# Soft-routed experts on one core: the first 512 rows of x by SP in float32, cast by ScalarE and VectorE

## The chip, the cores and the metric

The kernel runs on one core of a Trainium2 chip. Its engines are TensorE (PE: matmuls; PEld are its weight loads), VectorE (DVE), ScalarE (ACT), GpSimd (POOL) and SyncE (SP, which only issues DMAs). PE reads its operands from the on-chip memory SBUF and writes to PSUM, which has eight banks of 128 x 512 float32; DVE and ACT carry results from there. DMAs that SP issues go through the hardware queue q1, those that POOL issues through the software queue q0, for which POOL itself prepares the descriptors; only POOL's DMAs change the data type on the way. The metric is the device time in microseconds (us) of one execution.

## The reference, cut to what matters

```python
probs = softmax(router_logits)            # 16 x 512 tokens, 8 experts
output = zeros((16, 512, 2048))           # float32
for e in range(8):
    output += probs[:, :, e:e+1] * (x @ expert_weights[e])   # x: 512 columns, weights 512 x 2048
```

So every token's row of x is scaled by a probability and multiplied with each expert's weights; the eight products are summed.

## The kernel before

Tokens are taken flat, 8192 of them. The scaled rows z = p * x in float16, side by side for all experts, make one large matrix product, which the kernel computes with seven products in place of eight at two levels (Strassen's scheme in Winograd's form). A stage of it is `sub_product` (L370): for 256 rows at a time it multiplies sums of z blocks with sums of weight blocks and keeps the results in HBM; the last stage (from L607) puts the output together.

The change lies in the opening, before the first `sub_product`. There the kernel computes the first 512 rows' product with one quarter of the weights (`b11`, experts 0 to 3 and columns 0 to 1023) plainly:

- L94 to L104: DVE clears a tile, and PE runs 13 warm-up matmuls on zeros (`every`).
- L214 to L232: `xs0` is a float16 tile for 1024 rows of x, eight blocks of 128 x 512. `load_lg0(0)` brings the first logits by SP. `cast_x(0)` and `cast_x(2)` bring rows 0 to 255 and 512 to 767 by POOL, each one DMA from float32 in HBM to float16 in SBUF.
- L234 to L236: the identity matrix; POOL cuts it out of ones with `affine_select`.
- L237 to L245: POOL's queue then brings the weights `b11`: block (0,0) of expert 0 in two halves, the rest of the first three blocks in five DMAs of 512 KB (counted in float16), then `cast_x(4)`, `cast_x(6)`, then the fourth block. `behind()` keeps them after what was issued before on each engine's own queue.
- L247 to L274: `early_p` is the softmax of the first logits. `diag_e(e)` makes four diagonal matrices of expert e's probabilities, on DVE. `early_z0(e, d)` multiplies each 128-row block of xs0 with such a diagonal on PE, which transposes and scales it in one step: 4 blocks j of 4 matmuls, each block to one bank. `evacuate` casts the bank to the z tile `z0[j]`: DVE takes j = 0 and 2, ACT j = 1 and 3.
- L437 to L466: the order of the opening, which is kept as written for DVE and ACT (`keep_in_program_order` in the helper at L114):

```python
    ds_ = [diag_e(0), diag_e(1)]
    early_z0(0, ds_[0])
    ds_.append(diag_e(2))
    load_logits()
    early_z0(1, ds_[1])
```

After these lines come the two column halves n: for n = 0 the remaining `early_z0(2)` and `early_z0(3)` stand before the main matmuls of experts 0 and 1, and the main matmuls of expert e multiply z0[j][e] with the block `b11[e // 2, n]`. `load_logits` (L301) clears an element of each of two tiles on DVE, on which SP's loads of the other logits wait. SP carries one queue of its own; POOL issues its DMAs in the order of the text, and each waits until the DMA eight places ahead of it in POOL's queue has landed.

Of the kernel before, what the change touches and what calls it, by code (L numbers as in the profile page):

```python
# [32 lines left out]
def kernel(  # L33
# [7 lines left out]
    nc = tc.nc  # L41
    P = 128
    f16 = mybir.dt.float16
    f32 = mybir.dt.float32
# [3 lines left out]
    B, S, H = x.shape  # L48
# [7 lines left out]
    HQ = 256  # L56
# [4 lines left out]
    x_f = x.flatten_outer_dims()  # L61
# [4 lines left out]
    zpool = ctx.enter_context(tc.tile_pool(name="zpool", bufs=10))  # L66
# [44 lines left out]
    def note(i):  # L111
        last[i.ins.engine] = i.ins

    def dve(i):  # L114
        note(i)
        if pinned[0]:
            tc.keep_in_program_order(i)

    act = dve
# [12 lines left out]
    def sp(o, i):  # L132
        note(nc.sync.dma_start(out=o, in_=i))  # L133

    def pool(o, i):
        note(nc.gpsimd.dma_start(out=o, in_=i))  # L136
# [11 lines left out]
    def new_w():  # L148
        return wpool.tile([P, K8, NB], f16, name="w", tag="w")
# [64 lines left out]
    xs0 = new_w()  # L214

    ROWS = ("(p j) h -> p j h", "(j p) h -> p j h")

    def cast_x(j):
        pool(xs0[:, ds(j, 2), :], x_f[ds(j * HQ, HQ), :].rearrange(ROWS[j // 4], p=P))

    def load_lg0(t):
        rows = lg_f.rearrange("(q h) e -> q h e", h=2 * HQ)[ds(2 * t, 2), 0:HQ]
        tile_ = lg0[t].rearrange("p (q j) e -> p q j e", j=2)
        if t == 0:
            sp(tile_, rows.rearrange("q (p j) e -> p q j e", p=P))
        else:
            for q in range(2):
                sp(tile_[:, q], rows[q].rearrange("(j p) e -> p j e", p=P))
    lg0 = [cpool.tile([P, 4, E], f32, name=f"lg0_{t}") for t in range(2)]
    load_lg0(0)  # L230
    cast_x(0)
    cast_x(2)  # L232
    ident = cpool.tile([P, P], f16, name="ident")
    nc.vector.memset(ident, 1.0)  # L234
    nc.gpsimd.affine_select(out=ident, in_=ident, compare_op=mybir.AluOpType.is_equal, fill=0.0, base=0,
# [14 lines left out]
    def diag(p):  # L250

        d = h_tile([P, 4, P], f16)
        tt(d, ident.unsqueeze(1).to_broadcast([P, 4, P]), p.to_broadcast([P, 4, P]), MUL)
        return d
# [11 lines left out]
    def diag_e(e):  # L266
        return diag(ph0[0][:, e].unsqueeze(2))

    def early_z0(e, d):
        for j in range(4):  # L270
            ps = bank()
            for c in range(C):
                mm(ps[:, ds(c * P, P)], xs0[:, j, ds(c * P, P)], d[:, j], c == 0, c == C - 1)
            evacuate(z0[j][:, e], ps.rearrange("p (c t) -> p c t", c=C), j)  # L274
# [6 lines left out]
    def diag_j(j):  # L281
        return diag(ph0[1][:, :, ds(j % 4, 1)])
# [151 lines left out]
        except StopIteration as e:  # L434
            return e.value

    ds_ = [diag_e(0), diag_e(1)]  # L437
    early_z0(0, ds_[0])
    ds_.append(diag_e(2))
    load_logits()  # L440
# [1 line left out]
    for n in range(2):  # L442
# [19 lines left out]
        if n == 0:  # L462
            ph0.append(early_p(1))
            softmax_of_all()
            ds_ = [diag_j(j) for j in range(4, 8)]
# [293 lines left out]
```

## Time and profile before

| | us |
|---|---|
| time, median of 4 runs | 1433.92 (1433.35 to 1435.1) |
| the profiled execution's own time | 1434.07 |
| its span, first to last instruction | 1432.4 |
| PE busy | 1425.9 |
| DVE busy | 1031.8 |
| ACT busy | 270.5 |
| POOL busy | 220.1 |

The span is 1.7 us shorter than the time of the same execution: what lies before the first and after the last instruction is not in it. In the rows of the profile, L142 is the helper that issues every matmul but the warm-up, L122 that of every DVE operation on two tensors, L133 SP's DMAs, L136 POOL's loads, L260 and L258 the evacuations on DVE and ACT. A line of the timeline gives the start, the length, the engine, the line, the operation, the tiles (out<-in) and, in brackets, how long the engine had been idle and what ended that. A line of the chain of waits gives start, length and what the time went to.

### The profile page before, as it was taken

What the parts mean: (1) busy time and instruction counts of PE and PEld (TensorE: products, weight loads), DVE (VectorE), ACT (ScalarE), POOL (GpSimd) and SP (SyncE); (2) the same over time, 40 slices, a digit from 0 to 9 for tenths busy, and PEclk for the clock granted to TensorE, in tenths of its full rate; (3) what the DMA queues carried; (4) which work ended last, traced back from release to release, by engine and by line L of the source; (5) the groups of instructions that cost most, each with busy time, mean ns of one, the idle gap of its engine ahead of it and who ended that gap; (6) DMA issues with size and microseconds to landing.
All of it is one profiled execution on the core that took longest, in us unless ns stands there. A gap on an engine that the chain in (4) does not pass through costs nothing.

```text
span 1432.4 us, 18158 instructions
## 1 busy us (share of the span) xinstructions
PE 1425.9 (100%) x6649; PEld 647.6 (45%) x6649; DVE 1031.8 (72%) x1172; ACT 270.5 (19%) x471; POOL 220.1 (15%) x344
## 2 busy tenths in 40 slices
PE   9999999999999999999999999999999999999998
PEld 4444444444444444444444444444444444444443
DVE  6967585656686867766767687777777877877773
ACT  3211111111111111111111211111111111111111
POOL 3111000110001000001000222222222222222220
PEclk9999999999999999999999999999999999999999
DMA  9999967899649994368866967788777777778764
GB/s 194 187 248 268 274 162 190 183 248 270 207 149 303 352 331 153 132 190 221 214 250 205 298 198 233 235 242 236 228 224 220 214 214 213 226 234 242 220 199 103
DMA packets 191897, 318.92 MB, mean 223 GB/s; under 512 B 51648, under 2 KB 80320, under 8 KB 187200
## 3 DMA queue, kind: packets, MB, share of 16 engines
q1 hardware_dynamic: 135184, 202.92, 44.8%
q0 software_dynamic: 56624, 114.84, 34.1%
q8 instruction: 52, 0.85, 0.2%
q14 instruction: 37, 0.30, 0.1%
HBM read 180.13 MB, written 159.58 MB: 237 GB/s over the span
## 4 chain that ended last, share of the span: by engine, by line
PE 94%; issue 3%; DMA 1%; POOL 1%; DVE 1%; ACT 0%; POOLq 0%; SPq 0%; DVEq 0%; ACTq 0%
PE ps L142 93%; POOL out_dram L595 1%; DMA out_dram<-h 1%; DMA h<-kept 0%; PE every L104 0%; DVE h L122 0%; DVE z L122 0%; POOL w L136 0%; DVE z L260 0%; ACT ps L626 0%; SPq L133 0%; POOLq L595 0%; DVE h L101 0%; DVEq L122 0%; POOLq L136 0%
## 5 line engine op out<-in xcount | busy, mean ns | idle before, releaser
L142 PE MATMUL ps<-w,z 128*128 128x512 f16 x6552 | 1415.1, 379 | 0.6 <-DVE z L122 0.3
L142 PEld LDWEIGHTS <-z 128*128 128x128 f16 x6552 | 640.9, 98 | 773.4 <-DVE z L122 1.1
L122 DVE TENSOR_TENSOR h<-ps,h 128x512 f32<-128x512 f32 x389 | 267.7, 689 | 313.3 <-PE ps L142 90.7
L122 DVE TENSOR_TENSOR z<-xT,pT 128x2048 f16<-128x2048 f16 x252 | 304.1, 1218 | 33.8 <-PE ps L142 30.9
L122 DVE TENSOR_TENSOR z<-z 128x2048 f16<-128x2048 f16 x280 | 303.6, 1108 | 7.3
L404 ACT COPY h<-ps 128x512 f32<-128x512 f32 x248 | 145.4, 586 | 602.0 <-PE ps L142 593.1
L595 POOL DMA_DIRECT2D out_dram<-h x244 | 154.1, 664 | 533.0 <-DVE h L122 327.3
L122 DVE TENSOR_TENSOR w<-w 128x4096 f16<-128x4096 f16 x36 | 82.3, 2285 | 0.1
L662 ACT COPY h<-ps 128x512 f32<-128x512 f32 x64 | 37.5, 586 | 178.9 <-PE ps L142 176.0
L136 POOL DMA_DIRECT2D h<-in_x_dram x30 | 21.3, 711 | 270.4 <-DMA xT<-h 221.0
L122 DVE TENSOR_TENSOR h<-h,ps 128x512 f32<-128x512 f32 x77 | 52.5, 682 | 11.3 <-PE ps L142 10.2
L122 DVE TENSOR_TENSOR h<-h 128x512 f32<-128x512 f32 (+1 forms) x67 | 46.0, 687 | 18.4 <-DMA h<-kept 18.1
L136 POOL DMA_DIRECT2D w<-in_expert_weights_dram x41 | 30.7, 763 | 180.9 <-DVE w L161 128.2
L645 ACT ACTIVATE ps<-h 128x512 f32<-128x512 f32 x34 | 20.5, 602 | 160.8 <-DVE h L122 160.8
L626 ACT COPY ps<-h 128x512 f32<-128x512 f32 x64 | 35.5, 593 | 39.4 <-DMA h<-kept 30.3
L136 POOL DMA_DIRECT2D w<-wd x12 | 6.5, 545 | 189.5 <-DVE w L161 116.1
L722 ACT COPY h<-ps 128x512 f32<-128x512 f32 x15 | 8.8, 586 | 120.7 <-PE ps L142 120.7
L711 ACT COPY h<-ps 128x512 f32<-128x512 f32 x15 | 8.8, 586 | 16.4 <-PE ps L142 16.4
L260 DVE CAST z<-ps 128x512 f16<-128x512 f32 x8 | 5.1, 684 | 4.0 <-PE ps L142 4.0
L136 POOL DMA_DIRECT2D w<-wdt x8 | 4.4, 554 | 21.9 <-DVE w L161 21.9
L104 PE MATMUL every<-h 128*128 128x512 f16 x13 | 5.7, 632 | 1.3 <-DVE h L101 1.3
L142 PEld LDWEIGHTS <-w 128*128 128x128 f16 x80 | 5.0, 98 | 2.3 <-issue 0.8
(37 smaller groups left out, 42.7 us busy)
## 6 DMA issues: line engine op xcount, KB each, us to landing
out_dram<-h POOLq DMA_DIRECT2D x244, 256.0 KB, 4.9
kept<-h SPq DMA_DIRECT2D x192, 256.0 KB, 4.2
h<-kept SPq DMA_DIRECT2D x192, 256.0 KB, 4.5
pT<-p_dram SPq DMA_DIRECT2D x124, 256.0 KB, 5.1
w<-in_expert_weights_dram POOLq DMA_DIRECT2D x39, 512.0 KB, 12.9
out_dram<-h SPq DMA_DIRECT2D x76, 256.0 KB, 3.5
xT<-x SPq DMA_DIRECT2D x62, 256.0 KB, 2.9
w<-wd POOLq DMA_DIRECT2D x12, 1024.0 KB, 9.2
```

The lines of the kernel that those rows point to most:

```text
L104: nc.tensor.matmul(every[:, i % 8, :], zero[:, 0:P], zero, start=True, stop=True)
L122: dve(nc.vector.tensor_tensor(out=o, in0=a, in1=b, op=op))
L136: note(nc.gpsimd.dma_start(out=o, in_=i))
L142: nc.tensor.matmul(ps, z, w, start=start, stop=stop, skip_group_check=True)
L260: dve(nc.vector.tensor_copy(o, ps))
L404: nc.scalar.copy(t, ps)
L595: queue.dma_start(out=out_rows(self.q, odd, tn[0], cols, tn[1]), in_=o, **how)
L626: act(nc.scalar.copy(x, rows.m1[tn]))
L645: act(nc.scalar.mul(banks[b], v, scale))
L662: act(nc.scalar.copy(c21, x))
L711: act(nc.scalar.copy(r1, x))
L722: act(nc.scalar.copy(r3, x))
```

## The change

The two casting DMAs of POOL go. In their place SP loads the same 512 rows in float32 into two tiles `xf` (128 x 1024 each, out of the pool that also holds the z tiles), right after the first logits. ACT casts the first into `xs0`, ahead of all its evacuations; DVE casts the second, between the diagonals of experts 0 and 1. PE's instructions and their order stay as they are. POOL's first DMAs are the two halves of the first weight block; then follow the identity and the other weights, and all POOL's DMAs stand two places further ahead. On SP the two loads stand between the first logits and the rest of the logits' loads.

```diff
     load_lg0(0)
-    cast_x(0)
-    cast_x(2)
+    xf = [zpool.tile([P, 2, H], f32, name="xf", tag="z") for t in range(2)]
+    for t in range(2):
+        sp(xf[t], x_f[ds(2 * t * HQ, HQ), :].rearrange(ROWS[0], p=P))
     ident = cpool.tile([P, P], f16, name="ident")
...
-    ds_ = [diag_e(0), diag_e(1)]
+    act(nc.scalar.copy(xs0[:, 0:2], xf[0]))
+    ds_ = [diag_e(0)]
+    dve(nc.vector.tensor_copy(xs0[:, 2:4], xf[1]))
+    ds_.append(diag_e(1))
     early_z0(0, ds_[0])
     ds_.append(diag_e(2))
     load_logits()
```

## The prediction

> **What bounds the kernel now.** I read the page first: busy shares (section 1), then the chain that ended last (section 4).
>
> ```profile
> PE 1425.9 (100%) x6649; PEld 647.6 (45%) x6649; DVE 1031.8 (72%) x1172; ACT 270.5 (19%) x471; POOL 220.1 (15%) x344
> PE 94%; issue 3%; DMA 1%; POOL 1%; DVE 1%; ACT 0%; POOLq 0%; SPq 0%; DVEq 0%; ACTq 0%
> ```
>
> TensorE (PE) is busy for the whole span, so only a time in which PE stands still can be won, and every new one is paid in full. The change touches the first 10 us alone, so I asked for the chain of waits of the first 60 us (start, length, what):
>
> ```profile
> 1.30 5.74 PE every L104 x13
> 7.04 0.04 issue
> 7.08 0.40 PE ps L142 x4
> 7.48 0.02 issue
> 7.50 1.29 DVE z L260 x2
> 8.79 0.60 DVE h L122
> 9.39 0.01 DVE z L260
> 9.40 0.05 DVE lg L303
> 9.45 36.52 PE ps L142 x204
> 45.97 0.79 issue
> 46.76 1.23 DVE z L122
> ```
>
> The 13 warm-up matmuls on zeros hold PE until 7.04, whatever arrives before. Real work begins at 7.08, stops once, from 9.03 (7.08 plus the 1.95 us of the first 32 matmuls in the timeline) to 9.45, and then runs to 45.97. The stop is DVE's: two casts out of PSUM (1.29), the third diagonal (0.60), two small memsets (0.06). The next stop, 45.97 to 48.03, waits for DVE again, which works without a pause from 33.27, where it began on matmuls of PE: it moves with PE.
>
> Do x or the weights end a wait of PE? The timeline's issue times and the landing times of the DMA view for single issues say no:
>
> ```profile
> 1.35 1.26 POOL L136 DMA_DIRECT2D w<-in_x_dram  x2 [0.83 <-POOLq L743]
> 2.91 5.24 POOL L136 DMA_DIRECT2D w<-in_expert_weights_dram  x7
> 10.35 3.62 PE L142 MATMUL ps<-w,z 128*128 128x512 f16 x16
> ```
>
> ```profile
> w<-in_x_dram POOLq DMA_DIRECT2D x1, 256.0 KB, 4.1
> w<-in_x_dram POOLq DMA_DIRECT2D x1, 256.0 KB, 5.4
> w<-in_expert_weights_dram POOLq DMA_DIRECT2D x1, 256.0 KB, 6.5
> w<-in_expert_weights_dram POOLq DMA_DIRECT2D x1, 256.0 KB, 7.0
> ```
>
> The four rows are the first four issues, at 1.35, 2.02, 2.91 and 3.65. So x lands at 5.4 (needed at 7.08) and 7.46 (needed at 7.53, its ninth matmul); the first weights at 9.4 (needed at 10.35, 0.9 early) and 10.7 (needed at 12.08, half of those 16 matmuls later, 1.4 early). The next block (issued 4.37) lands at 13.2 and its matmuls start at 14.70; the slack of those behind it is no smaller. Weights that come sooner end no wait.
>
> **The change part by part.** *Removed:* two casting DMAs from POOL, 1.26 us of descriptor work, so the seven weight issues begin at 1.35 instead of 2.91. Value: nothing, since nothing waits for them; the cover is the 0.9 us above, and it only grows. POOL keeps the mask for the identity (0.34 us) after two issues, as before, so the first diagonal at 4.08 stays.
>
> *Added on SP:* two issues between the first logits (0.82) and the second part of the other logits. An issue here takes 0.455 us, so they start near 1.33 and 1.85. Behind them stands one small logits DMA, which lands 3.6 in the profile and is needed at 16.4; a delay of 1 us costs nothing.
>
> *Added on ScalarE:* a cast of 128x1024. Its rows go from 0.40 (256 elements, L311) to 0.63 (512, L200), so 0.63 + 2 x 0.23 = 1.09 us. Its first half of x is issued at 1.33; an SP load of 256 KB lands 2.9 after its issue (the page's section 6, xT<-x), and 512 KB need 256 KB more, 0.7 us at the 352 GB/s of the page's best slice: about 4.9, cast by 6.0. PE wants it at 7.08: hidden, with 1 us of cover. What is queued behind the waiting cast on ScalarE are the evacuations, first needed at 7.73.
>
> *Added on VectorE:* the cast of the second half, and here is the cost. It stands between the first and the second diagonal, and behind it on DVE come diagonal 2, both evacuations, diagonal 3 and the memsets that release the logits. Before, DVE was idle from 5.37 (4.08 + 1.29, two diagonals) to 7.50. Now the evacuations start at L + 0.03 + c + 0.65, where L is the landing, c the cast and 0.65 half of the two diagonals' 1.29, unless that is before 7.50. Everything after 7.50 is the old chain, so PE's loss is d = L + c + 0.68 - 7.50, not below 0.
>
> c: no row has an SBUF-to-SBUF cast on DVE. Below: an f16 product of 2048 elements takes 1.22, so 0.61 for 1024. Above: twice the 0.68 of a 512-element cast from PSUM, 1.37. The nearest row is that cast, f32 to f16: two in succession take 1.29. I take 1.29.
>
> L: alone on the DMA engines, 1 MB needs 1.33 + 2.9 + 0.75 MB at 352 GB/s (2.2) = 6.4; with the best 256 KB row (2.5) and 400 GB/s, 5.8. But weights now move beside it: they take x's old place at POOL, whose first packets came near 2.5. If both queues share evenly from there, 1 MB of x and 1 MB of weights at 400 GB/s end at 2.5 + 5.2 = 7.7. In the old order the software queue came up slowly (70 GB/s in the stretch from 2 to 4 us, 197 from 4 to 6), which favours x early on. I take L = 6.4, between 5.8 and 7.7.
>
> d = 6.4 + 1.29 + 0.68 - 7.50 = 0.9 us. Bounds: 5.8 + 0.61 + 0.68 gives 0; 7.7 + 1.37 + 0.68 gives 2.25. Nothing takes a loss back: PE is dense from 9.45, and the DVE work that ends the stop at 45.97 starts from PE at 33.27. So 1434.07 (the profiled execution: span 1432.4 and 1.7 around it) + 0.9 = 1434.9; the median of the runs shown is 0.15 lower, so **1434.8**.
>
> *A rule against the change.* POOL is at its descriptors without a break from 2.66 to 8.84 in the profile, so the new cast falls among them. The Trainium skill ("SBUF — State Buffer", Who interferes with whom) says that a VectorE copy or cast between SBUF tiles in a two-port mode and a GpSimd instruction exclude each other, the later one waiting for the whole of the other. By it the cast would wait up to one POOL issue, 0.7 to 0.8 us, and the sum would be up to 0.8 higher; no row here has such a pair. The same skill ("DMA: Bandwidth & Descriptors", Issuing engines are not separate DMA queues) says that SP's and POOL's transfers interleave on the same 16 engines; the rows agree in one place, where 48 KB issued on SP at 23.7 landed 6.7 us later beside the weights. By it L would be the even share, 7.7, and the loss 2.2.
>
> **The rivals.**
> 1. *Fully hidden.* If L + c is at most 6.8 (x at 6.2 with the fast cast, at 5.5 with the slow one), the cast fits into DVE's 2.13 us of idle time and d = 0: 1433.9. For it: the slow start of the software queue. Against: the 1 MB alone needs 5.8 to 6.4.
> 2. *Slower than before.* The second half of x is held up behind the weights' packets. Logits of 64 KB issued on SP at 9.44 took 4.7 us; of the four stores of 48 KB from 23.65 on (p_dram) the first took 6.7 and the median is 8.8. With 6.7, L = 1.85 + 6.7 = 8.55 and d = 8.55 + 1.29 + 0.68 - 7.50 = 3.0; with 8.8, 5.1. It decides from L + c = 9.7 on. PE would then stand for 3 us right after its warm-up, which ran at one matmul per 0.44 us (5.74/13) against 0.216 later (715.03/3312), though the page's row of granted clock is full from the start; if it fell back to the slow rate, each 3 us of work would cost 3 us again. 1437 to 1440, at 1438. Against: the weights' queue is still empty when SP issues at 1.33 and 1.85, whereas those rows met a full one.
> 3. *Faster.* PE's stop at 9.03 to 9.45 is the only one that the change could close: 1433.5 at the most, and DVE's chain behind the 7.50 start has lost no instruction. More than that needs PE to start before 7.04, which the warm-up forbids.
> 4. *The weights don't come sooner* because the DMA engines are shared: the bytes read are the same. Nothing waits for them, so the time is that of the forecast.
>
> **How the numbers follow.** Forecast, d from 0.1 to 2.25: 0.60 (rival 4 lies in it). Hidden: 0.15. Slower by rival 2: 0.20, all of it beyond 0.2%. Rival 3: 0.05, of which 0.03 beyond. 0.2% is 2.9 us, about what a measurement of this kernel can tell from no change. So faster 0.03, same 0.77, slower 0.20. The range goes from rival 3's 1433.4 to 1437.5, which holds the bounds (1433.9 to 1436.2) and the nearer half of a quarter of rival 2.
>
> **What would show it.** Right: xf landing near 5 and 6.4; a DVE cast of about 1.3 us that ends after 7; PE's two stops, at 7.5 and 9, together about 0.9 us longer; the first weights landing before 9 and PE's first 512-column matmul near 11.2 without waiting for them; the rest of the timeline shifted by the same amount. Wrong: PE waiting for a weight block; xf landing after 8.5; warm matmuls at 0.43 us spacing after 7; or the evacuations still at 7.50.

## The result, and the profile after

The changed kernel takes 1436.25 us (median of 37 runs, 1435.02 to 1439.12) against 1434.41 for the kernel before (57 runs, 1433.35 to 1436.09): a ratio of 1.0013, 95% interval 1.0008 to 1.0018, that is 1.1 to 2.6 us slower (1.84 between the medians). It lies in the range that was forecast and inside the 0.2% that was called no change; the loss of 0.9 us that was forecast was too small.

The page of the changed kernel (section 1, the chain by engine) shows nothing:

```profile
PE 1425.0 (99%) x6649; PEld 647.3 (45%) x6649; DVE 1032.0 (72%) x1173; ACT 271.9 (19%) x472; POOL 218.7 (15%) x342
PE 93%; issue 3%; DMA 2%; POOL 1%; DVE 1%; SPq 0%; ACT 0%; POOLq 0%; DVEq 0%; ACTq 0%
```

The chain of waits of its first 60 us (start, length, what) shows it all:

```profile
1.83 5.95 DMA xf<-in_x_dram
7.77 0.02 issue
7.80 0.69 DVE w L440
8.49 0.60 DVE h L122
9.09 1.20 DVE z L261 x2
10.29 0.60 DVE h L122
10.89 0.01 DVE z L261
10.90 0.05 DVE lg L304
10.95 36.52 PE ps L142 x204
47.47 0.78 issue
48.25 1.23 DVE z L122
```

Before, this chain began with the warm-up matmuls. Now it begins with SP's second load: the second half of x lands at 7.77, and cast, second diagonal, two evacuations and third diagonal follow on VectorE. PE resumes at 10.95 instead of 9.45, 1.50 us later than in the profile of before; the 36.52 us of dense matmuls and the stop behind them are the same to 0.02. The timeline of PE shows where the time is lost (start, length; in brackets the idle time and what ended it):

```profile
1.29 4.50 PE L104 MATMUL every<-h 128*128 128x512 f16 x13 [1.29 <-DVE h L101]
5.86 0.62 PE L142 MATMUL ps<-h,w 128*128 128x128 f16 x8
8.55 1.65 PE L142 MATMUL ps<-h,w 128*128 128x128 f16 x24 [2.06 <-DVE w L440]
10.95 1.07 PE L142 MATMUL ps<-h,w 128*128 128x128 f16 x16 [0.75 <-DVE lg L304]
11.85 3.62 PE L142 MATMUL ps<-w,z 128*128 128x512 f16 x16
```

In this execution the 13 warm-up matmuls took 4.50 us, not 5.74: PE was ready at 5.79, did eight small matmuls and stood for 2.06 us. The loads themselves, the first at 1.34 and the second at 1.83, took these times to land (the DMA view, for the first issue alone and for both), where the casting DMAs had taken 4.1 and 5.4:

```profile
xf<-in_x_dram SPq DMA_DIRECT2D x1, 512.0 KB, 3.4
```

```profile
xf<-in_x_dram SPq DMA_DIRECT2D x2, 512.0 KB, 4.7
```

The second row is the middle of the two, 3.4 and 5.9.

Not all of the loss lies inside the span. The time less the span of the same execution, 1.7 us before, has the median 1.95 us over the runs of the changed kernel, so some 0.24 of the 1.84 us lies ahead of the first instruction or behind the last.

### The profile page after: what moved, and what is told of

Its sections match the earlier page's. It is cut to its first block, busy times and chain, and to the rows that moved or that the text cites. A ratio compares the mean times of both kernels' runs of the same rounds, so it can differ in the third digit from the quotient of the medians.

```text
span 1434.3 us, 18161 instructions
## 1 busy us (share of the span) xinstructions
PE 1425.0 (99%) x6649; PEld 647.3 (45%) x6649; DVE 1032.0 (72%) x1173; ACT 271.9 (19%) x472; POOL 218.7 (15%) x342
## 4 chain that ended last, share of the span: by engine, by line
PE 93%; issue 3%; DMA 2%; POOL 1%; DVE 1%; SPq 0%; ACT 0%; POOLq 0%; DVEq 0%; ACTq 0%
PE ps L142 93%; POOL out_dram L599 1%; DMA out_dram<-h 1%; DMA h<-kept 0%; DMA xf<-in_x_dram 0%; DVE h L122 0%; DVE z L122 0%; POOL w L136 0%; SPq L133 0%; DVE z L261 0%; DVE w L440 0%; ACT ps L630 0%; POOLq L599 0%; DVEq L122 0%; POOLq L136 0%
## 5 line engine op out<-in xcount | busy, mean ns | idle before, releaser
L142 PE MATMUL ps<-h,w 128*128 128x128 f16 x64 | 4.4, 219 | 2.9 <-DVE w L440 2.1
```

Source lines behind the costliest of these rows:

```text
L142: nc.tensor.matmul(ps, z, w, start=start, stop=stop, skip_group_check=True)
```

## The experiments

The theory (A): the loss is one chain, the late landing L of the second half of x, because the weights now move beside it, and the VectorE work queued behind it. Rivals: the order on VectorE doesn't matter and the loss sits on SP's queue or in later stages (B); 1 MB through SP's queue is that slow by itself (D). A further stop of PE, near 842 us where the output stage begins and ScalarE waits for a load of kept results, had gone from 0.27 to 0.86 us of idle time between the two profiles, so chance had to be told from effect there.

### The second diagonal ahead of the cast

```diff
-    ds_ = [diag_e(0)]
+    ds_ = [diag_e(0), diag_e(1)]
     dve(nc.vector.tensor_copy(xs0[:, 2:4], xf[1]))
-    ds_.append(diag_e(1))
```

> The changed kernel with VectorE's cast moved behind the second diagonal; nothing else. Theory A (the loss is one chain: the second half of x lands late because the weights move beside it, then the cast, the second diagonal, two evacuations and the third diagonal follow one another on VectorE): x lands at 7.8 as before, the second diagonal is done by 5.6, the cast runs 7.8 to 8.5, and PE resumes after its second stop near 10.35 instead of 10.95; the time falls by 0.6 us against the changed kernel, to 1435.6 to 1435.8. Rival B (the loss does not hang on VectorE's order in the opening, but on SP's queue and on the stage that puts the output together): PE resumes at 10.9 and the time stays at 1436.2.

Measured: 1435.31 us, ratio to before 1.0007 (0.9998 to 1.0016); the interval holds a time 0.6 us below the changed kernel's, and also no difference from it, so the profile has to decide. The chain:

```profile
1.83 6.01 DMA xf<-in_x_dram
...
7.86 0.69 DVE w L440
8.56 1.20 DVE z L261 x2
9.76 0.60 DVE h L122
...
10.41 36.52 PE ps L142 x204
```

The same landing, the same cast, one link of 0.60 less, and PE resumes at 10.41, 0.54 earlier. The chain is what A says; B's claim that VectorE's order doesn't matter falls.

### No weights beside x

```diff
     b11 = {kn: new_w() for kn in BLOCKS}
+    held = cpool.tile([P, 1], f32, name="held")
+    note(nc.gpsimd.tensor_copy(out=held, in_=xf[1][:, 0, 0:1]))
```

> The changed kernel, with a one-column copy of the second half of x on GpSimd ahead of the weights' DMAs, so that no weights move until x has landed. Theory A (L is late because of sharing): x lands at 5.8 to 6.4 instead of 7.8, the third diagonal is done by 9.5 and PE resumes there; the first weights, issued near 6.3, land at 10.4 (4.1 us as for the first DMA of an empty software queue) to 12.8 (6.5 us), so that PE waits 0 to 2.4 us for them; time 1434.4 to 1437. Theory D (1 MB in float32 through SP's queue takes so long by itself): x still lands at 7.4 to 7.8, and the weights come at 12 or later; time 1437 to 1439.

The chain:

```profile
1.83 4.78 DMA xf<-in_x_dram
6.61 0.06 issue
6.67 0.64 POOL held L240
7.31 4.49 DMA w<-in_expert_weights_dram
11.80 0.05 issue
11.85 37.32 PE ps L142 x188
```

The second half lands at 6.61, not at 7.77, so the weights beside it cost 1.2 us of L, and A's bounds for 1 MB alone (5.8 to 6.4) were 0.2 too low; D falls. The bytes of the two queues show when the weights cost it (DMA view; MB, POOL's counted in float16):

| stretch, us | SP's queue, changed kernel | POOL's queue, changed kernel | SP's queue, no weights beside x |
|---|---|---|---|
| 2 to 4.75 | 0.61 | 0.06 | 0.59 |
| 4.75 to 6 | 0.27 | 0.07 | 0.47 |
| 6 to 7.77 | 0.19 | 0.17 | x has landed at 6.61 |

Until 4.75 the weights cost x nothing, since hardly any of them moved. After that x moved at about half its rate alone, and from 6 on slower still. (The other two profiles of the changed kernel, below, have 0.59 and 0.53 MB of x in the first stretch, 0.24 and 0.27 in the second.)

PE resumed behind its second stop at 9.78. The time, 1437.03 us, ratio 1.0014 (1.0005 to 1.0023), isn't told apart from the changed kernel's: what x gains, the weights lose, since the first of them, issued at 7.31, landed at 11.80 and PE waited for them. And in the profiled execution, the slowest of eleven at 1438.93 us, PE paid once more, as the table by stretches shows (stretch, its length, busy time and count of PE, PEld, DVE, ACT, POOL, granted clock, DMA share, GB/s):

```profile
6.41:11.85 5.44, 3.34 (x49) 2.73 (x49) 5.22 (x11) 3.32 (x6) 5.18 (x7) 1.00 0.52 76
11.85:15.30 3.45, 3.45 (x9) 1.25 (x10) 0.89 (x2) 0.00 (x0) 3.01 (x5) 0.51 1.10 174
15.30:19.00 3.70, 3.70 (x31) 2.16 (x30) 1.54 (x4) 1.07 (x2) 0.75 (x1) 1.00 1.25 222
```

After a stretch in which PE stood for 2.1 of 5.4 us the granted clock fell to 0.51 for 3.4 us. The first 16 large matmuls took 5.31 us instead of 3.62, and the opening ends 1.69 us later than in the changed kernel, though both started those matmuls at 11.85. Most executions don't pay this: seven of the eleven have a mean granted clock of 1.000, where a fall of this length would leave 0.999.

### Half of the change

The first half of x by SP and ScalarE, the second by POOL with the cast in the DMA, ahead of the weights; no cast on VectorE.

```diff
-    for t in range(2):
-        sp(xf[t], x_f[ds(2 * t * HQ, HQ), :].rearrange(ROWS[0], p=P))
+    sp(xf[0], x_f[ds(0, HQ), :].rearrange(ROWS[0], p=P))
+    cast_x(2)
...
-    ds_ = [diag_e(0)]
-    dve(nc.vector.tensor_copy(xs0[:, 2:4], xf[1]))
-    ds_.append(diag_e(1))
+    ds_ = [diag_e(0), diag_e(1)]
```

> Half of the change: the first half of x through SP in float32 with ScalarE's cast, the second half by POOL with the cast in the DMA, ahead of the weights; no cast on VectorE. Theory A: the first half lands at 4.7 to 5.4, the second at 5.5 to 6.5 (4.1 us from its issue at 1.35, with up to 1 us for sharing), neither is late, VectorE's chain starts as early as PE lets it, PE resumes from its second stop at 8.5 to 9.45 and the time is 1433.6 to 1434.5, not slower than before. Rival B (what costs is SP's float32 load or what follows in the later stages): 1435.3 to 1436.3.

```profile
1.34 3.93 DMA xf<-in_x_dram
5.27 0.02 issue
5.29 1.05 ACT w L438
6.34 0.05 issue
6.39 0.41 PE ps L142 x4
...
6.83 1.29 DVE z L261 x2
8.12 0.60 DVE h L122
...
8.77 36.52 PE ps L142 x204
```

PE resumes at 8.77, 2.2 us ahead of the changed kernel and 0.7 ahead of the first profile of before. The time, 1433.79 us, has the ratio 0.9994 (0.9985 to 1.0003): faster than the changed kernel, whose interval lies wholly above, and not shown to be faster than before. One float32 load by SP costs nothing that shows; what costs is the second one, with what hangs on it.

### Both kernels again

The kernel before three times more, the changed one twice more, for what varies.

> The kernel before, unchanged, looked at once more, for what varies from one execution to the next. Theory A: the warm-up matmuls end anywhere from 5.8 to 7.1 (the changed kernel's 13 took 4.5 us against 5.73), PE resumes at 9.0 to 9.45 all the same, because the second half of x lands at 7.5, and PE's stop at the start of the output stage (0.43 us in one profile, 1.03 in the other) lies anywhere between these. If the stop there is the change's work, it is 0.4 again.

> The kernel before, unchanged. Two questions: where PE stands at the end of the opening (its stop near 48 us ended at 48.03 and 48.23 in two profiles), and how long it stands before the output stage near 842 us (0.43 us and nothing). If the latter is chance of the DMAs, it lies anywhere from 0 to 1.9 here; if it belongs to the kernel, it is 0 to 0.5 again.

> The kernel before once more, with the same two questions: 48.0 to 48.3 at the end of the opening; before the output stage 0 to 1.9 us by chance, or 0 to 0.5 if the short stop belongs to the kernel.

> The changed kernel, unchanged. The opening's stop ends at 49.5 again (49.53 and, with both casts on VectorE, 49.52), whatever the warm-up takes, since the second half of x lands at 7.8. The stop before the output stage: by chance 0 to 1.9 us; if it belongs to the kernel, 0.8 to 1.1 as in the two profiles (1.03, 0.98).

> The changed kernel once more: 49.5 at the end of the opening; before the output stage 0 to 1.9 us by chance, or 0.8 to 1.1 if it belongs to the kernel.

| profile | first real matmul | second half of x landed | PE resumes behind its stop near 10 us | PE resumes behind the stop near 48 us | idle before the output stage | time |
|---|---|---|---|---|---|---|
| before, 1 | 7.08 | 7.46 | 9.45 | 48.03 | 0.27 | 1434.07 |
| before, 2 | 5.84 | 6.90 | 8.73 | 48.23 | none | 1433.86 |
| before, 3 | 7.08 | 6.73 | 9.53 | 48.43 | 0.44 | 1434.65 |
| before, 4 | 6.13 | 7.14 | 8.97 | 47.81 | 1.70 | 1435.29 |
| changed, 1 | 5.86 | 7.77 | 10.95 | 49.53 | 0.86 | 1436.31 |
| changed, 2 | 6.28 | 7.75 | 10.92 | 49.50 | 0.33 | 1435.81 |
| changed, 3 | 7.08 | 7.91 | 11.08 | 49.66 | 0.17 | 1435.68 |

What was expected of the changed kernel's opening held; the kernel before varied more than was expected of it, with x in as early as 6.73, PE back as early as 8.73, and the opening's end from 47.81 to 48.43. The opening ends at 48.1 before (mean of four) and at 49.6 after (mean of three): 1.44 us, whether the warm-up ends early or late. The idle time before the output stage (as the view gives it; the stops of 0.43 and 1.03 in the expectations count 0.16 more) goes from 0 to 1.70 in one kernel and from 0.17 to 0.86 in the other, so nothing ties it to the change. Each row's time, less the end of the opening and this idle time, is 1385.63 to 1385.78 before and 1385.85 to 1385.98 in the changed kernel: these two stops explain most of what varies.

The rows of before held a surprise. In three of its four profiles PE waited for weights, here the second one (PE's timeline):

```profile
5.84 0.61 PE L142 MATMUL ps<-h,w 128*128 128x128 f16 x8
6.94 1.51 PE L142 MATMUL ps<-h,w 128*128 128x128 f16 x24 [0.50 <-DMA w<-in_x_dram]
8.73 1.07 PE L142 MATMUL ps<-h,w 128*128 128x128 f16 x16 [0.27 <-DVE lg L303]
10.13 3.63 PE L142 MATMUL ps<-w,z 128*128 128x512 f16 x16 [0.34 <-DMA w<-in_expert_weights_dram]
18.35 1.89 PE L142 MATMUL ps<-w,z 128*128 128x512 f16 x8 [0.25 <-DMA w<-in_expert_weights_dram]
```

The warm-up ended at 5.79, PE waited for the second half of x, then for the first weights, and at 18.35 for a later block. Of the four, only the profile that the prediction was made from had all its weights early.

### Both casts on VectorE

```diff
-    act(nc.scalar.copy(xs0[:, 0:2], xf[0]))
+    dve(nc.vector.tensor_copy(xs0[:, 0:2], xf[0]))
```

> The changed kernel with both casts on VectorE; the first then falls among POOL's descriptor work (3.28 to 7.07 in the changed kernel's profile). If a two-port cast and GpSimd exclude each other, as the one-column copy of the run with x alone suggests (on GpSimd 0.70 us long, from 6.67 to 7.37, beside the cast from 6.63 to 7.32), then either the first cast starts up to 0.8 us after the landing, or takes 0.69 and a POOL issue beside it takes up to 1.5 in place of 0.80. If they do not, the cast takes 0.69 and each POOL issue 0.75 to 0.82. For the chain of theory A nothing changes: the second half of x still lands near 7.8 and PE resumes near 10.9.

PE resumed at 10.94, as in the changed kernel. The casts, and POOL's five issues from 3.27 to 7.14, amid which the first of them stands (duration in ns, least, median, most):

```profile
L136 POOL DMA_DIRECT2D w<-in_expert_weights_dram x5: 760/802/894, 3.3 to 6.4; - x5
L438 DVE CAST w<-xf x1: 911/911/911, 5.2 to 5.2; 128x1024 f16<-128x1024 f32 x1
L440 DVE CAST w<-xf x1: 694/694/694, 7.8 to 7.8; 128x1024 f16<-128x1024 f32 x1
```

The cast at 5.18, amid the issues, took 0.91 us, the one at 7.79, when POOL was idle but for the first 0.05 us, 0.69. Of the two issues that ran beside the first cast, one took 0.89 against a median of 0.80; but an issue of 0.88 stands in the changed kernel too, at 1.36, with no cast beside it. So the cast was slowed by 0.2 us, the issue by 0.1 at most, and neither waited for the whole of the other: neither expectation holds.

### The third diagonal ahead of the evacuations

With half of the change (first expectation), with the kernel before (second), and with the mirror of half the change (third: first half of x by POOL, second by SP and ScalarE).

```diff
-    ds_ = [diag_e(0), diag_e(1)]
+    ds_ = [diag_e(0), diag_e(1), diag_e(2)]
     early_z0(0, ds_[0])
-    ds_.append(diag_e(2))
```

> The kernel with half of the change (first half of x by SP, second by POOL), with the third diagonal computed ahead of the evacuations. Theory A: VectorE has 1.3 us of idle time there, so the stop of 0.42 us before the third group of small matmuls goes, PE's first 512-column matmul starts at 9.25 instead of 9.67, the first weights have landed by 8.2 and hold nothing up; time 0.4 us less than with half of the change, 1433.2 to 1433.6, if the stop before the output stage is the same. Rival E (the opening is hidden behind the stop before the output stage, which is set by DMAs): the marker moves and the time does not, 1433.6 to 1434.

> The kernel before with the third diagonal ahead of the evacuations, nothing else. If no weights are waited for (my prediction), PE's first 512-column matmul starts at 8.7 to 9.9 instead of 9.6 to 10.35, and the time falls by 0.4 us to 1434.0. If the first weights are late in the kernel before, as in its second profile (landed at 10.09, PE starts on them at 10.13), the marker stays at 9.5 to 10.3 by them, and the gain is 0 to 0.4 us: 1434.0 to 1434.4.

> The mirror of half the change, with the third diagonal ahead: the first half of x by POOL with the cast in the DMA, the second half by SP in float32, cast by ScalarE. Theory A: the first half lands at 5.5 to 6.5 and PE starts there, the second is cast by 6.4 to 6.6, later than its ninth small matmul needs it by 0 to 0.5 us; PE's first 512-column matmul starts at 8.8 to 9.3, the time is 1433.2 to 1433.7. Rival B (SP's float32 load costs as such): 1434.5 or more.

Times: 1434.05, 1434.36 and 1433.95 us; ratios to before, whose median was 1434.70 in these rounds, 0.9995 (0.9986 to 1.0004), 1.0001 (0.9991 to 1.0010) and 0.9996 (0.9987 to 1.0005). None is shown to be faster than before, and the first and the third missed the 1433.2 to 1433.7 that was expected of them. The chain of the third kernel up to the stop near 48:

```profile
1.30 5.55 PE every L104 x13
6.84 0.04 issue
6.89 38.29 PE ps L142 x236
```

Here, and with half of the change, PE has no stop at all between the warm-up and 45 us, and resumes behind the stop near 48 at 47.24 and 47.52. The first 512-column matmul started at 9.56 and 9.85, later than expected, only because the warm-ups of these two executions ended at 6.84 and 7.04. In the kernel before, the same edit only uncovers the next wait (the 48 small matmuls now stand in one row, and then the first weights are late):

```profile
6.62 2.84 PE L142 MATMUL ps<-h,w 128*128 128x128 f16 x48
10.06 3.63 PE L142 MATMUL ps<-w,z 128*128 128x512 f16 x16 [0.60 <-DMA w<-in_expert_weights_dram]
```

So once x isn't late, weights that come sooner seem to be worth something: the opening ends 0.3 to 0.9 us sooner (47.24 and 47.52 against 47.82 and 48.1). That this reaches the time isn't shown: those two profiles stood 1.37 and 1.56 us before the output stage. In all the profiles here, the five with the earliest openings, 47.82 or sooner, stood 1.25 to 1.70 us there, and the later ones 0 to 0.86, but for 1.76 in the run without weights beside x. So the rival that such a gain is lost again before the output stage (E) stays open. It doesn't touch the loss of the changed kernel, whose opening ends later than any of before.

## Why the prediction was right or wrong, point by point

- **The mechanism and its sign: right.** The loss sits on VectorE's chain behind L: 1.50 us of it is seen in the pair of profiles, 1.44 between the means at the end of the opening. "Nothing takes a loss back" was not quite so: where PE resumes near 10 us the means are 1.81 apart (9.17 and 10.98), and the kernel before loses the other 0.37 later, to its own waits for weights.
- **The 1.7 us around the span, taken as unchanged: a second term.** The time less the span is 1.71 us in the median of the kernel before, 1.95 in the changed kernel, 1.95 and 1.93 in the first two experiments, with both loads on SP, and 1.76 to 1.79 in the three with one. The 1.44 of the opening and this 0.24 come to 1.68 of the measured 1.84 (1.1 to 2.6); the rest is within the noise. What the 0.24 is, the record doesn't show.
- **L, taken as 6.4, was 7.75 to 7.91: the term that was mis-sized.** The step that failed: since the software queue's slow start "favours x early on", L was left at the sum for x alone, with no price for the sharing. Alone, x landed at 6.61. The slow start was real, it left the engines to x until 4.75; but x was not in by then, and the rest of it came 1.2 us later beside the weights.
- **The even share, 7.7, came so near by luck.** It had 1 MB of weights beside 1 MB of x at 400 GB/s. Measured from 2 to 7.77 us, x and the small logits had 1.07 MB, the weights 0.30 MB (counted in float16), and the traffic was 237 GB/s: x had more than half, of much less.
- **c, taken as 1.29, was 0.69**, near the lower bound: a cast from PSUM is a poor row for one between SBUF tiles. With the measured L and c the sum is 7.77 + 0.69 + 0.68 - 7.50 = 1.64; the two evacuations, back to back, took 1.20 and not 1.29, and the second diagonal 0.60 and not 0.65, which makes it the 1.50. The two errors, +1.4 and -0.6, hid each other in part: that the forecast came within a microsecond is luck to that extent.
- **"The 13 warm-up matmuls on zeros hold PE until 7.04, whatever arrives before": wrong.** The first real matmul started anywhere from 5.84 to 7.08 where nothing held it. The loss is the same, since PE then waits for x in place of the warm-up, but the cover of ScalarE's cast (1 us in the forecast) was gone in the changed kernel's second profile: PE stood 0.69 us for it, ahead of the longer wait.
- **"Weights that come sooner end no wait": wrong for most executions.** Three of four profiles of before have such waits, 0.1 to 0.6 us of idle time in all. The conclusion held for the changed kernel only because x was later still.
- **The two issues on SP, POOL's start, the small logits load.** The issues began at 1.34 and 1.83 for 0.45 us each and POOL's at 1.36, as forecast. The logits behind them landed at 9.07, 5.4 us later than in the profile of before, where a delay of 1 us had been reckoned with; they are needed so late that nothing noticed.
- **The rule on GpSimd and VectorE:** its price, up to 0.8 us, was not paid. POOL was idle for all but the last 0.08 us of the second cast, and where a cast met its issues the cast lost 0.2.
- **Rivals:** the hidden case failed by L. The starved case did not come, L stayed 0.6 below its 8.55. Its second half, the fall to the slow rate, is real (the run without weights beside x), but the three profiles of the changed kernel don't have it; its two slowest runs, 1438.97 and 1439.12 us, have no trace, so whether the clock fell there isn't known. Rival 3's stop of 0.42 us can indeed be closed, by moving the third diagonal, not by this change.

## What to carry to other kernels

A load that moves to another queue is not out of the way of what it was queued behind: it shares the DMA engines, so put a price on the sharing (1.2 us on 1 MB here), and give the urgent half the early place. A cast that leaves the DMA goes onto an engine's queue, and every instruction behind it waits for the landing; put what does not need the data ahead of the wait. Slack of less than 1 us read from one profile is no cover: read several executions before calling a transfer early enough.

## What the runs showed of the hardware

- The same 13 warm-up matmuls took from 4.30 to 5.73 us in profiles of the two kernels. They start 0.43 us apart at first and 0.22 apart later; the trace's record of the granted clock begins, at full, where that changes, from 4.0 to 7.3 us after the start (ahead of it there is no record, and the views print 1.00). The Trainium skill ("TensorE: Matmul & The Clock Gate", Part 1: The HAM clock gate) says that activity is judged in free-running windows of some 3.4 us, so that the same kernel warms up at different points; these runs agree.
- In the run without weights beside x the clock stood at half for 3.4 us, from 11.90, which is the length of one such window, after PE had stood for 2.1 of 5.4 us in pauses of 1.00 at most. With 2.06 and 0.75 us of idle time between 5.86 and 10.95 in the changed kernel's first profile it did not fall. What decides between the two isn't shown.
- A 128x1024 cast from float32 to float16 between SBUF tiles takes 0.69 us on VectorE and 1.05 on ScalarE.
- Beside POOL's descriptor work the same VectorE cast takes 0.91 us. The Trainium skill ("SBUF — State Buffer", Who interferes with whom) has the later of the two wait for the whole of the other; in the one meeting here the cast lost 0.22 us and the issue 0.09 at most, so the rule isn't met in full. In the run without weights beside x, a one-column copy on GpSimd took 0.70 us beside such a cast, from 6.67 to 7.37 against 6.63 to 7.32, which would fit the rule; how long that copy takes alone was not measured.
